# An encoder block with two attentions on one core: a hand-written VectorE order, a later meta product, another order of pair products, and keys and queries loaded a head ahead

## The chip, the cores and the metric

The kernel runs on one core of one Trainium2 chip. The metric is the device time of one execution in microseconds (us). A core has a matrix engine (PE, with its weight loads listed apart as PEld), three engines for elementwise work (DVE is VectorE, ACT is ScalarE, POOL is GpSimd) and a queue engine (SP) that issues all loads and stores here. The engines run side by side and wait for one another by semaphores; each takes its own instructions in a fixed order.

## The reference

One block of an encoder with 1024 tokens, 16 meta tokens ahead of them, and 1024 features, in fp32. Cut to its core:

```python
h = concat(meta, x)                                   # 1040 x 1024
proj = rms_norm(h, norm_mix) @ w_in                   # qa ka va | qb kb vb | ga gb
# differential attention: 4 heads, two maps each, values of 128, all 1040 keys
attn = softmax(q1 k1 + bias) - lam * softmax(q2 k2 + bias)
y_a  = rms_norm(attn @ v, subln_g) * (1 - lambda_init)
# windowed attention: 8 heads in 2 groups, a block of 128 queries sees its own block,
# one to either side, and the 16 meta keys; a sink logit joins the denominator
y_b  = softmax_with_sink(qb kb + bias) @ vb
h = h + (sigmoid(ga) * (y_a @ w_ba) + sigmoid(gb) * (y_b @ w_bb)) @ w_o
n = rms_norm(h, norm_ffn)
h = h + (silu(n @ w_g) * (n @ w_u)) @ w_d             # 2816 hidden features
out = rms_norm(h, norm_final)[meta:]
```

## The kernel before

Every fp32 operand of a product is kept as two fp32r tiles, a rounded high part and the rest (`split`, L120 to L122: ACT writes the high part, L121; POOL or DVE the low part, L122). A product is three matmuls: high by high, high by low, low by high. Matmuls have at most 512 columns.

The work around the change falls into four stages, in order of time.

**Window attention** (L320 to L390, up to about 245 us). For each group and block of 128 queries `attend_b` makes the scores (`bps`, two matmuls for each of four heads, L331), and a generator `values` makes the transposes (`bpt`, L365), their splits (`btr`: ACT L367, DVE L369), the products with the values (`bpy`, L359) and the result (ACT L380, DVE L381). The last step of `values` is the product with the 16 meta values and the result. PE's order is written out by hand here: the string `SLOTS_B` is gone through once for each block, and takes a score step ("s"), a step of `values` of the block before ("t"), the last step of `values` of the block before that ("y"), or a step of three matmuls of other projections (`more`, made by `fill_b`, "g").

**Sums for the pair products** (about 230 to 272 us). Some projections are done in pairs of 128-column blocks and two halves of the tokens and features, by a seven-product scheme in place of eight. Products 5, 6, 7 and 4 need sums of normalised inputs: `token_sums(u)` makes, for each of four groups of 128 tokens in either half, four sums of high and low part (`f`, L620), four differences (L622 to L625), and four splits into `tops` (ACT high, DVE low, L122). Meanwhile PE runs the rest of `more`. The order on DVE, ACT, POOL and SP is chosen here by the framework's scheduler.

**Pair products** (L655 to L718, about 260 to 360 us). A unit is one pair of column blocks: units 0 and 1 are the queries of the differential attention, 2 to 4 are gates. `steps_t` lists (unit, product) in PE's order, written by hand. `weights_t` makes the weight sums (`s1` and the in-place differences in `wt`, L667 to L671, DVE) and splits them into `wop_t` (ACT, POOL), up to four products ahead. `product_t` runs 12 matmuls (`pt`, L697) into a PSUM bank. Products 1, 6, 7, 4 go into one bank and 5, 3 into another, 2 into a third, each adding to what stands there. After 1, 5 and 6 ACT copies the bank (`u`, L701); after 2, 7 and 3 DVE adds the bank to a copy (L706). The results of units 0 and 1 are split once more (`qk_stage`: ACT L235, DVE L236), stored, and loaded again by the heads; those of the gates are stored.

**Heads** (L760 to L935, about 366 to 640 us). For 4 heads and 8 tiles of 128 queries: `load_a` (at a head's first tile) issues on SP the loads of the second map's queries and keys (L768, L769, L771), the first map's, and the values. `scores_a` makes scores (`aps`, L792) for the second map and then the first, with minimum, exponential and combination on DVE, ACT and POOL (L795 to L806); `turn` transposes two tiles later (`apt`, L818; split L820 to L822); `values_a` and `normed_a` make products with the values (`apy`, L831) and the norm (`apst`, `af`, `apf`, L844 to L852). The order on PE is again by hand: `SLOTS` for the first `N_MORE` tiles, `SLOTS_LAST` for the others, with "s" a score step, "t" a transpose step, "n" a step of the values or the norm, "g" a step of three matmuls of the gate projections that are left (`fill(1)`). `G_FIRST` steps run at the start, `G_HEAD` at each new head, and `HOLD` steps are kept for the end, where `while tail` runs the last values with three gate steps each.

Results of gate projections are stored by SP (L748); SP takes its instructions in order, so a store that waits holds what stands behind it.

Of the kernel before, what the change touches and what calls it, by code (L numbers as in the profile page):

```python
# [39 lines left out]
PC_BUFS = 8  # L40
PAD_T = 192
COMBINE_POOL = (0, 1, 2, 3)
SLOTS = "stgstgstgsngsnsn"
SLOTS_LAST = "stgstgstsngsnsn"
N_MORE = 13
S_BUFS = (2, 2)
AT_BUFS = 2
G_BUFS = 3
HOLD = 39
PAIRS = 3  # L50
HEADS_EARLY = 3
GT_BUFS = 4
WB_BUFS = 5
G_HEAD = 7
G_FIRST = 33

QK_BUFS = 3
W_BUFS = 2
# [2 lines left out]
V_AT = 2  # L61
S_BUFS_B = 3
B_FIRST = 6
SLOTS_B = "ysgtgsgtgtsgtgtsgtgt"
E_STEPS = 1
OP_BUFS = 8
RING_RAW = 5
# [12 lines left out]
def encoder_block(ctx: ExitStack, tc: tile.TileContext, x, meta, norm_mix, w_in, lq1, lk1, lq2, lk2,  # L80
# [7 lines left out]
    def f32(ap):  # L88
        return ap.bitcast(F32)
# [520 lines left out]
    def quad(t, kh, th, u):  # L610
        return t[:, 4 * kh:4 * kh + 4, th * 512 + u * P:th * 512 + u * P + P]

    def token_sums(u):

        cols = slice(u * P, u * P + P)
        tt = nc.vector.tensor_tensor
        f = {}
        for kh, th in ((0, 0), (0, 1), (1, 1), (1, 0)):
            f[kh, th] = pc_tile(f"f{kh}{th}_{u}").rearrange("p (c t) -> p c t", c=4)
            tt(f[kh, th], f32(quad(hT_hi, kh, th, u)), f32(quad(hT_lo, kh, th, u)), ALU.add)  # L620
        b11, b12, b21, b22 = f[0, 0], f[0, 1], f[1, 0], f[1, 1]
        tt(b12, b12, b11, ALU.subtract)  # L622
        tt(b22, b22, b12, ALU.subtract)
        tt(b11, b22, b11, ALU.subtract)
        tt(b21, b21, b22, ALU.subtract)  # L625
        for p, src in ((6, b22), (5, b12), (7, b11), (4, b21)):
            split(tops[p][:, 0, :, cols], tops[p][:, 1, :, cols], src, nc.vector)

    def moving(p, c, b):
        if p in tops:  # L630
# [2 lines left out]
        return (hT_hi, hT_lo)[b][:, 4 * kh + c, th * 512:th * 512 + 512]  # L633


    for _ in more:
        pass
    flush_v()
    for u in range(4):
        token_sums(u)  # L640
    close_psum1()
    psum_t, close_psum_t = pool("psum_t", space=PSUM)
    psum1 = psum_t
# [2 lines left out]
    units = [[C_QA + (2 * i + k) * P for k in range(2)] for i in range(2)]  # L646
    units += [gate_cols[2 * i:2 * i + 2] for i in range(PAIRS)]
    steps_t = [(u, p) for u in range(2) for p in (1, 2)]
    steps_t += [(u, p) for u in range(2) for p in (6, 5, 7, 3, 4)]
    steps_t += [(u, p) for u in range(2, len(units)) for p in (1, 2, 6, 5, 7, 3, 4)]  # L650
    raw_t, s1_t, ops_t, ps_t, u_t = {}, {}, {}, {}, {}

    def load_t(u):
# [6 lines left out]
    def weights_t(u, p):  # L660
        tt = nc.vector.tensor_tensor
        a11, a12 = (raw_t[u, kh][:, :, 0:P] for kh in range(2))
        a21, a22 = (raw_t[u, kh][:, :, P:2 * P] for kh in range(2))
        if p == 6:

            s1_t[u] = tpool.tile([P, 4, P], F32, tag="s1", name=f"s1_{u}", bufs=2)
            tt(s1_t[u], a21, a22, ALU.add)  # L667
            tt(a21, a11, a21, ALU.subtract)
            tt(a11, s1_t[u], a11, ALU.subtract)
        elif p == 3:  # L670
            tt(a12, a12, a11, ALU.subtract)  # L671
        src = s1_t.pop(u) if p == 5 else {1: a11, 2: a12, 6: a11, 7: a21, 3: a12, 4: a22}[p]
        op = wpool.tile([P, DC, P], F32R, tag=("wh", "wl")[len(ops_t) % 2], name=f"wop_t{u}_{p}", bufs=W_BUFS)
        ops_t[u, p] = op
        split(op[:, 0:4], op[:, 4:8], src, nc.gpsimd)
# [14 lines left out]
    def product_t(u, p):  # L690
        op, key = ops_t[u, p], (u, {1: 1, 6: 1, 7: 1, 4: 1, 2: 2, 5: 3, 3: 3}[p])
        if p in (1, 2, 5):
            ps_t[key] = pp_bank(f"pt_{u}_{p}")
        ps = ps_t[key]
        for c in range(4):
            for n, (a, b) in enumerate(((0, 0), (0, 1), (1, 0))):
                nc.tensor.matmul(ps, op[:, 4 * a + c], moving(p, c, b), start=(p in (1, 2, 5) and c == 0 and n == 0),  # L697
                                 stop=(p in (4, 2, 3) and c == 3 and n == 2), skip_group_check=True)
        if p in (1, 5, 6):
            u_t[u, p] = pc_tile(f"u{p}_{u}")  # L700
            nc.scalar.copy(u_t[u, p], ps)  # L701
        elif p == 4:
            result_t(u, 1, 0, ps, True)
        else:
            other = u_t.pop((u, {2: 1, 7: 5, 3: 6}[p]))
            nc.vector.tensor_tensor(other, ps, other, ALU.add)  # L706
            result_t(u, *{2: (0, 0), 7: (1, 1), 3: (0, 1)}[p], other)

    for u in range(3):
        load_t(u)  # L710
# [48 lines left out]
    for i in range(2):  # L759
        nc.gpsimd.memset(s0s[i][:, L + 2 * NM:], 0.0)  # L760

    def load_a(h):
        p = apool
        qs, ks = [None, None], [None, None]
        for m in (1, 0):
            q = qs[m] = p.tile([P, S], F32R, tag=f"q{m}", name=f"aq{h}_{m}")
            k = ks[m] = p.tile([P, 2, L], F32R, tag=f"k{m}", name=f"ak{h}_{m}")
            nc.sync.dma_start(f32(q), qa_d[h][m])  # L768
            nc.sync.dma_start(f32(k)[:, 0, :], ka_d[h][m])  # L769
            for hl in range(2):  # L770
                nc.sync.dma_start(f32(k)[64 - 64 * hl:128 - 64 * hl, 1, :], ka_d[h][m, 64 * hl:64 * hl + 64, :])  # L771
        v = p.tile([P, 2, 9, P], F32R, tag="v", name=f"av{h}")
        nc.gpsimd.memset(f32(v)[:, 0, 8, :], 0.0)
        nc.sync.dma_start(f32(v)[:, :, 0:8, :], va_d[h][:, :, 0:8, :])
        nc.sync.dma_start(f32(v)[:2 * NM, 0, 8, :], va_d[h][:2 * NM, 0, 8, :])
        nc.sync.dma_start(f32(v)[2 * NM:3 * NM, 0, 8, :], va_d[h][:NM, 1, 8, :])
        return qs, ks, v
# [102 lines left out]

    order_pe = tc.manual_schedule(engines={mybir.EngineType.PE})
    order_pe.__enter__()
    tiles, turning, tail = [], iter(()), []

    def step_tail():
        while tail and next(tail[0], True):
# [2 lines left out]
    for n in range(AH * NT + T_LAG):  # L889
        scoring, turning = iter(()), iter(())  # L890
        if n < AH * NT:
            h, t = divmod(n, NT)
            if t == 0:
                ld = load_a(h)
                if not h:
                    fill(G_FIRST)
            if t % 2 == 0:
                at_ = apool.tile([P, 9, 2, 256], F32R, tag="at", name=f"at{h}_{t}", bufs=AT_BUFS)
            s = [None, None]
            tiles.append((h, t, s, at_, ld[2]))  # L900
            scoring = scores_a(h, t, ld, s)
        if n >= T_LAG:
            turning = turn(tiles[n - T_LAG])
        if n in (NT, 2 * NT, 3 * NT):

            fill(G_HEAD - 3)
            for _ in turning:
                pass
            step_tail()
            fill(3)  # L910
        for what in SLOTS if n < N_MORE else SLOTS_LAST:
            if what == "s":
                next(scoring, None)
            elif what == "t":
                next(turning, None)
            elif what == "n":
                step_tail()
            else:
                fill(1)
        for _ in scoring:  # L920
            pass
        for _ in turning:
            pass
        if n in (1, 2):
            fill(3)
        if n >= T_LAG and tiles[n - T_LAG][1] % 2:
            tail.append(later(tiles[n - T_LAG]))
    n_gates[0] += HOLD
    while tail:
        step_tail()  # L930
        fill(3)
    order_pe.__exit__(None, None, None)
    close_apool()
    fill(1000)
# [604 lines left out]
```

## Time and profile before

| | |
|---|---|
| median of 3 runs | 1493.73 us (1493.52 to 1493.82) |
| the profiled execution | 1494.14 us, span 1492.4 us |
| PE busy | 1443.1 us, 97% of the span |
| DVE, ACT, POOL busy | 892.0, 687.9, 562.7 us |
| HBM read, written | 131.24 MB, 53.94 MB |

The span runs from the first to the last recorded instruction; the time of the execution is somewhat longer. Times in the trace are counted from the start of the span. A row of a timeline gives the start, the duration, the engine, the line of the kernel, the operation with output and inputs, and how many instructions of that kind follow each other; in brackets stands how long the engine was idle just before and what released it. A matmul's end is modelled, so that consecutive matmuls overlap in such rows. A row of waits gives the engine, what it wanted to run, whose instruction it waited for, the total, the number of times and the longest.

### The profile page before, as it was taken

The page shows a single profiled execution, that of the slowest core. Times are in us where ns is not written, and L with a number is a line of the kernel's source. Part 1 is how long each engine was busy: PE and PEld are TensorE (multiplying, and loading weights), DVE is VectorE, ACT ScalarE, POOL GpSimd, SP SyncE. Part 2 cuts the span into 40 slices and gives each one's busy share as a digit, 9 for nine tenths or more (in the row PEclk, how much of TensorE's full clock was granted, in tenths as well). Part 3 has the DMA queues.
Part 4 walks back from the last instruction along what each step waited for, and adds up shares of the span by engine and source line. Part 5 has one row for each costly group of instructions (what it writes and reads, how often), then busy time and mean ns, then how long its engine had stood idle before and what let it go on. Part 6 is the DMA issues. An engine that isn't in the chain of part 4 may idle for free.

```text
span 1492.4 us, 21014 instructions
## 1 busy us (share of the span) xinstructions
PE 1443.1 (97%) x7315; PEld 1228.8 (82%) x7315; DVE 892.0 (60%) x1635; ACT 687.9 (46%) x1296; POOL 562.7 (38%) x556
## 2 busy tenths in 40 slices
PE   8999998999999999999999999999999999999997
PEld 7988888788889898878888878888888888888886
DVE  6466668621768786813432586655555554778567
ACT  6366663432555565625533463333333333444444
POOL 4253433543332232313763325544455453000344
PEclk9999999899999999999999999999999999999999
DMA  7423324434542414147653244322333332864433
GB/s 235 90 81 105 93 79 136 134 106 126 160 130 78 122 65 144 42 146 227 206 183 113 90 126 145 124 98 98 104 106 107 106 106 106 309 224 131 134 123 139
DMA packets 154203, 193.13 MB, mean 129 GB/s; under 512 B 16288, under 2 KB 98656, under 8 KB 154096
## 3 DMA queue, kind: packets, MB, share of 16 engines
q1 hardware_dynamic: 154096, 191.78, 40.8%
q8 instruction: 58, 0.95, 0.3%
q14 instruction: 49, 0.40, 0.1%
HBM read 131.24 MB, written 53.94 MB: 124 GB/s over the span
## 4 chain that ended last, share of the span: by engine, by line
PE 77%; DMA 7%; DVE 5%; issue 4%; POOL 4%; ACT 2%; SPq 1%; POOLq 0%; ACTq 0%; DVEq 0%
PE pg L1320 28%; PE pd L1414 8%; PE pt L697 6%; PE po L1086 6%; PE pp_g L215 5%; PE aps L792 4%; PE ppa L735 4%; PE apy L831 3%; DMA ak<-ka_d 3%; POOL oa L122 3%; PE pp_qb L215 3%; PE apt L818 2%; PE bpt L365 1%; PE pp_ka L215 1%; PE pp_va L215 1%
## 5 line engine op out<-in xcount | busy, mean ns | idle before, releaser
L1320 PE MATMUL pg<-t,wop 128*128 128x512 f32 x1056 | 243.0, 389 | 1.6 <-DVE wop L122 1.6
L1320 PEld LDWEIGHTS pg<-t,wop 128*128 128x128 f32 x1056 | 198.1, 188 | 43.3 <-DVE wop L122 2.0
L122 POOL TENSOR_TENSOR wop<-wf,wop 128x512 fp32r<-128x512 f32 x118 | 158.6, 1347 | 155.3 <-ACT wop L121 141.0
L1414 PE MATMUL pd<-ob,oa 128*128 128x512 f32 x924 | 210.2, 389 | 0.9 <-DVE ob L122 0.5
L1414 PEld LDWEIGHTS pd<-ob,oa 128*128 128x128 f32 x924 | 173.3, 188 | 37.6 <-DVE ob L122 0.9
L1320 PE MATMUL pg<-b,wop 128*128 128x512 f32 x792 | 183.2, 389 | 0.0
L1320 PEld LDWEIGHTS pg<-b,wop 128*128 128x128 f32 x792 | 148.5, 188 | 30.7
L121 ACT ACTIVATE wop<-wf 128x512 fp32r<-128x512 f32 x128 | 80.3, 632 | 83.1 <-PE pg L1320 51.9
L800 ACT ACTIVATE as<-as,amn 128x1040 f32<-128x1040 f32 x64 | 74.6, 1165 | 74.8 <-DVE amn L795 65.9
L122 POOL TENSOR_TENSOR oa<-ra,oa 128x512 fp32r<-128x512 f32 x33 | 44.0, 1335 | 170.8 <-ACT oa L121 169.4
L792 PE MATMUL aps<-ak,aq 128*128 128x352 f32 (+1 forms) x384 | 91.9, 331 | 10.1 <-DMA ak<-ka_d 8.5
L121 ACT ACTIVATE oa<-ra 128x512 fp32r<-128x512 f32 x77 | 48.7, 632 | 107.7 <-PE pd L1414 51.9
L1086 PE MATMUL po<-woh,mT 128*128 128x512 f32 x384 | 88.6, 390 | 0.0
L792 PEld LDWEIGHTS aps<-ak,aq 128*128 128x128 f32 x384 | 66.9, 190 | 23.7 <-issue 6.8
L188 POOL TENSOR_TENSOR wl_c<-w_c,wh_c 128x512 fp32r<-128x512 f32 x48 | 61.1, 1295 | 61.7 <-ACT wh_c L185 61.7
L1086 PEld LDWEIGHTS po<-woh,mT 128*128 128x128 f32 x384 | 71.7, 188 | 14.7
L1144 DVE TENSOR_TENSOR s<-wf,wf 128x512 f32<-128x512 f32 x22 | 16.5, 752 | 109.0 <-DMA wf<-in_w_ff_up_dram 54.5
L122 POOL TENSOR_TENSOR wop_t<-wt,wop_t 128x512 fp32r<-128x512 f32 x30 | 46.6, 1557 | 63.7 <-ACT wop_t L121 62.2
L345 POOL TENSOR_SCALAR bs<-bs,bdn 128x432 f32<-128x432 f32 (+1 forms) x64 | 36.9, 596 | 89.0 <-DVE bdn L343 57.8
L215 PE MATMUL pp_g<-hT_hi,wh_c 128*128 128x512 f32 x160 | 68.7, 430 | 0.0
L803 POOL TENSOR_SCALAR as<-as,adn,neglam 128x1040 f32<-128x1040 f32 x32 | 38.9, 1215 | 73.2 <-DVE adn L801 68.8
L215 PE MATMUL pp_g<-hT_hi,wl_c 128*128 128x512 f32 x160 | 63.3, 395 | 0.0
(279 smaller groups left out, 3173.5 us busy)
## 6 DMA issues: line engine op xcount, KB each, us to landing
ra<-aop SPq DMA_DIRECT2D x77, 256.0 KB, 2.6
w_c<-in_w_in_dram SPq DMA_DIRECT2D x25, 512.0 KB, 4.3
wf<-in_w_ff_gate_dram SPq DMA_DIRECT2D x24, 512.0 KB, 3.6
wf<-in_w_ff_up_dram SPq DMA_DIRECT2D x24, 512.0 KB, 3.5
aop<-as SPq DMA_DIRECT2D x44, 256.0 KB, 2.1
aop<-c SPq DMA_DIRECT2D x33, 256.0 KB, 2.0
gt<-g_d SPq DMA_DIRECT2D x32, 256.0 KB, 3.2
wt<-in_w_in_dram SPq DMA_DIRECT2D x10, 512.0 KB, 4.6
```

What stands on the lines that cost most here:

```text
L121: nc.scalar.activation(hi, src, AF.Copy)
L122: lo_eng.tensor_tensor(lo, src, f32(hi), ALU.subtract)
L188: (lo_eng or nc.gpsimd).tensor_tensor(wl[:, c], w[:, c], f32(wh[:, c]), ALU.subtract)
L215: nc.tensor.matmul(ps[:, :n], a[:, c, :], b[:, c, at:at + n], start=(c == 0 and i == 0), stop=(c == DC - 1 and i == 2))
L697: nc.tensor.matmul(ps, op[:, 4 * a + c], moving(p, c, b), start=(p in (1, 2, 5) and c == 0 and n == 0), stop=(p in (4, 2, 3) and c == 3 an ...
L735: nc.tensor.matmul(ps, w[:, a, j, :], src(j, b, tk), start=(j == 0 and n == 0), stop=(j == 3 and n == 2))
L792: nc.tensor.matmul(ps[:, :n], qs[m][:, t * P:(t + 1) * P], ks[m][:, vv, k0:k0 + n], start=(vv == 0), stop=(vv == 1))
L800: nc.scalar.activation(s[m][:, 0:L], s[m][:, 0:L], AF.Exp, bias=low, scale=-1.0, accum_out=dn[:, m:m + 1])
L831: nc.tensor.matmul(py[:, cols], v[:kp, a, k, :], at_[:kp, k, b, :], start=(k == 0 and j == 0), stop=(k == 8))
L1086: nc.tensor.matmul(ps, mT[:, c, a, t * P:(t + 1) * P], wos[q, c][:, b], start=(c == 0 and n == 0), stop=(c == DC - 1 and n == 2))
L1320: nc.tensor.matmul(ps, op[:, x, c, :], b[:, y, c, :], start=(p in (1, 2, 5) and c == 0 and n == 0), stop=(p in (4, 2, 3) and c == 3 and n ...
L1414: nc.tensor.matmul(ps[u], oa[:, a, u * P:(u + 1) * P], ob[:, b, :], start=(p in (1, 2, 5) and j == 0 and k == 0), stop=(p in (2, 3, 4) and ...
```

## The change

- In the window stage the string of slots has the last values step ("y") behind the first score step and the first projection step, no longer ahead of them.
- `token_sums` becomes a generator of single DVE operations. DVE's order is written out by hand for this stretch: one operation of the sums after each of three in four steps of `more`, and the rest behind. The splits run in the order 5, 6, 7, 4.
- The pair products run 5, 3 and then 6, 7, 4. For units 0 and 1 the two 5, 3 pairs come first. The sums and differences of weights that were made at product 6 are made at product 5. The result that was formed after product 3 is formed after product 6, from the bank of 5 and 3 and the copy of 6.
- `load_qk` loads one map's queries and keys. The second map's tiles have two buffers, and those of the next head are loaded at a head's fifth tile; the first map's and the values are loaded at the head's first tile as before.
- The slot strings of the heads have their values steps at the end; `SLOTS` holds for 4 tiles and no longer for 13; three more gate steps run at the start, seven more are kept for the end. The kept steps are released at the last tile of queries, three run beside each of the two last transposes, and two instead of three beside each last values step.

```diff
--- before.py
+++ after.py
@@ -40,19 +40,19 @@
 PC_BUFS = 8
 PAD_T = 192
 COMBINE_POOL = (0, 1, 2, 3)
-SLOTS = "stgstgstgsngsnsn"
-SLOTS_LAST = "stgstgstsngsnsn"
-N_MORE = 13
+SLOTS = "stgstgstsgsgsnnn"
+SLOTS_LAST = "stgstgstsgssnnn"
+N_MORE = 4
 S_BUFS = (2, 2)
 AT_BUFS = 2
 G_BUFS = 3
-HOLD = 39
+HOLD = 46
 PAIRS = 3
 HEADS_EARLY = 3
 GT_BUFS = 4
 WB_BUFS = 5
 G_HEAD = 7
-G_FIRST = 33
+G_FIRST = 36
 
 QK_BUFS = 3
 W_BUFS = 2
@@ -61,7 +61,7 @@
 V_AT = 2
 S_BUFS_B = 3
 B_FIRST = 6
-SLOTS_B = "ysgtgsgtgtsgtgtsgtgt"
+SLOTS_B = "sgytgsgtgtsgtgtsgtgt"
 E_STEPS = 1
 OP_BUFS = 8
 RING_RAW = 5
@@ -613,18 +613,22 @@
     def token_sums(u):
 
         cols = slice(u * P, u * P + P)
-        tt = nc.vector.tensor_tensor
+
+        def tt(*args):
+            nc.vector.tensor_tensor(*args)
+
         f = {}
         for kh, th in ((0, 0), (0, 1), (1, 1), (1, 0)):
             f[kh, th] = pc_tile(f"f{kh}{th}_{u}").rearrange("p (c t) -> p c t", c=4)
             tt(f[kh, th], f32(quad(hT_hi, kh, th, u)), f32(quad(hT_lo, kh, th, u)), ALU.add)
+            yield
         b11, b12, b21, b22 = f[0, 0], f[0, 1], f[1, 0], f[1, 1]
-        tt(b12, b12, b11, ALU.subtract)
-        tt(b22, b22, b12, ALU.subtract)
-        tt(b11, b22, b11, ALU.subtract)
-        tt(b21, b21, b22, ALU.subtract)
-        for p, src in ((6, b22), (5, b12), (7, b11), (4, b21)):
+        for out, x, y in ((b12, b12, b11), (b22, b22, b12), (b11, b22, b11), (b21, b21, b22)):
+            tt(out, x, y, ALU.subtract)
+            yield
+        for p, src in ((5, b12), (6, b22), (7, b11), (4, b21)):
             split(tops[p][:, 0, :, cols], tops[p][:, 1, :, cols], src, nc.vector)
+            yield
 
     def moving(p, c, b):
         if p in tops:
@@ -633,11 +637,16 @@
         return (hT_hi, hT_lo)[b][:, 4 * kh + c, th * 512:th * 512 + 512]
 
 
-    for _ in more:
+    order_dve = tc.manual_schedule(engines={mybir.EngineType.DVE})
+    order_dve.__enter__()
+    sums = chain.from_iterable(token_sums(u) for u in range(4))
+    for i, _ in enumerate(more):
+        if i % 4 < 3:
+            next(sums)
+    flush_v()
+    for _ in sums:
         pass
-    flush_v()
-    for u in range(4):
-        token_sums(u)
+    order_dve.__exit__(None, None, None)
     close_psum1()
     psum_t, close_psum_t = pool("psum_t", space=PSUM)
     psum1 = psum_t
@@ -646,8 +655,9 @@
     units = [[C_QA + (2 * i + k) * P for k in range(2)] for i in range(2)]
     units += [gate_cols[2 * i:2 * i + 2] for i in range(PAIRS)]
     steps_t = [(u, p) for u in range(2) for p in (1, 2)]
-    steps_t += [(u, p) for u in range(2) for p in (6, 5, 7, 3, 4)]
-    steps_t += [(u, p) for u in range(2, len(units)) for p in (1, 2, 6, 5, 7, 3, 4)]
+    steps_t += [(u, p) for u in range(2) for p in (5, 3)]
+    steps_t += [(u, p) for u in range(2) for p in (6, 7, 4)]
+    steps_t += [(u, p) for u in range(2, len(units)) for p in (1, 2, 5, 3, 6, 7, 4)]
     raw_t, s1_t, ops_t, ps_t, u_t = {}, {}, {}, {}, {}
 
     def load_t(u):
@@ -661,7 +671,7 @@
         tt = nc.vector.tensor_tensor
         a11, a12 = (raw_t[u, kh][:, :, 0:P] for kh in range(2))
         a21, a22 = (raw_t[u, kh][:, :, P:2 * P] for kh in range(2))
-        if p == 6:
+        if p == 5:
 
             s1_t[u] = tpool.tile([P, 4, P], F32, tag="s1", name=f"s1_{u}", bufs=2)
             tt(s1_t[u], a21, a22, ALU.add)
@@ -699,12 +709,12 @@
         if p in (1, 5, 6):
             u_t[u, p] = pc_tile(f"u{p}_{u}")
             nc.scalar.copy(u_t[u, p], ps)
-        elif p == 4:
+        if p == 4:
             result_t(u, 1, 0, ps, True)
-        else:
-            other = u_t.pop((u, {2: 1, 7: 5, 3: 6}[p]))
-            nc.vector.tensor_tensor(other, ps, other, ALU.add)
-            result_t(u, *{2: (0, 0), 7: (1, 1), 3: (0, 1)}[p], other)
+        elif p in (2, 6, 7):
+            other = u_t.pop((u, {2: 1, 6: 6, 7: 5}[p]))
+            nc.vector.tensor_tensor(other, ps_t[u, 3] if p == 6 else ps, other, ALU.add)
+            result_t(u, *{2: (0, 0), 7: (1, 1), 6: (0, 1)}[p], other)
 
     for u in range(3):
         load_t(u)
@@ -759,16 +769,18 @@
     for i in range(2):
         nc.gpsimd.memset(s0s[i][:, L + 2 * NM:], 0.0)
 
-    def load_a(h):
+    def load_qk(h, m):
+        q = apool.tile([P, S], F32R, tag=f"q{m}", name=f"aq{h}_{m}", bufs=1 + m)
+        k = apool.tile([P, 2, L], F32R, tag=f"k{m}", name=f"ak{h}_{m}", bufs=1 + m)
+        nc.sync.dma_start(f32(q), qa_d[h][m])
+        nc.sync.dma_start(f32(k)[:, 0, :], ka_d[h][m])
+        for hl in range(2):
+            nc.sync.dma_start(f32(k)[64 - 64 * hl:128 - 64 * hl, 1, :], ka_d[h][m, 64 * hl:64 * hl + 64, :])
+        return q, k
+
+    def load_a(h, first):
         p = apool
-        qs, ks = [None, None], [None, None]
-        for m in (1, 0):
-            q = qs[m] = p.tile([P, S], F32R, tag=f"q{m}", name=f"aq{h}_{m}")
-            k = ks[m] = p.tile([P, 2, L], F32R, tag=f"k{m}", name=f"ak{h}_{m}")
-            nc.sync.dma_start(f32(q), qa_d[h][m])
-            nc.sync.dma_start(f32(k)[:, 0, :], ka_d[h][m])
-            for hl in range(2):
-                nc.sync.dma_start(f32(k)[64 - 64 * hl:128 - 64 * hl, 1, :], ka_d[h][m, 64 * hl:64 * hl + 64, :])
+        qs, ks = zip(load_qk(h, 0), first)
         v = p.tile([P, 2, 9, P], F32R, tag="v", name=f"av{h}")
         nc.gpsimd.memset(f32(v)[:, 0, 8, :], 0.0)
         nc.sync.dma_start(f32(v)[:, :, 0:8, :], va_d[h][:, :, 0:8, :])
@@ -880,7 +892,7 @@
 
     order_pe = tc.manual_schedule(engines={mybir.EngineType.PE})
     order_pe.__enter__()
-    tiles, turning, tail = [], iter(()), []
+    tiles, turning, tail, ahead = [], iter(()), [], None
 
     def step_tail():
         while tail and next(tail[0], True):
@@ -891,14 +903,18 @@
         if n < AH * NT:
             h, t = divmod(n, NT)
             if t == 0:
-                ld = load_a(h)
+                ld = load_a(h, ahead or load_qk(h, 1))
                 if not h:
                     fill(G_FIRST)
+            if t == 4 and h < AH - 1:
+                ahead = load_qk(h + 1, 1)
             if t % 2 == 0:
                 at_ = apool.tile([P, 9, 2, 256], F32R, tag="at", name=f"at{h}_{t}", bufs=AT_BUFS)
             s = [None, None]
             tiles.append((h, t, s, at_, ld[2]))
             scoring = scores_a(h, t, ld, s)
+        if n >= AH * NT:
+            fill(3)
         if n >= T_LAG:
             turning = turn(tiles[n - T_LAG])
         if n in (NT, 2 * NT, 3 * NT):
@@ -923,12 +939,13 @@
             pass
         if n in (1, 2):
             fill(3)
+        if n == AH * NT - 1:
+            n_gates[0] += HOLD
         if n >= T_LAG and tiles[n - T_LAG][1] % 2:
             tail.append(later(tiles[n - T_LAG]))
-    n_gates[0] += HOLD
     while tail:
         step_tail()
-        fill(3)
+        fill(2)
     order_pe.__exit__(None, None, None)
     close_apool()
     fill(1000)
```

## What is predicted

> **What bounds the kernel now.** I read the page's head and busy times first, then the waits of TensorE (PE), then the windows of the three stages that the change touches, then the timeline at the longest waits. The page, its span and its first busy line:
>
> ```profile
> span 1492.4 us, 21014 instructions
> PE 1443.1 (97%) x7315; PEld 1228.8 (82%) x7315; DVE 892.0 (60%) x1635; ACT 687.9 (46%) x1296; POOL 562.7 (38%) x556
> ```
>
> PE sets the time: 1492.4 − 1443.1 = 49.3 us of idle is all that reordering can win, except for what the clock gives. The change alters no matmul count, so I count only idle time removed and added, and half-clock time. The waits of PE over the whole run (us in total, times, longest):
>
> ```profile
> PE aps L792 <- DMA ak<-ka_d: 8.5, 8, 1.7
> PE bpy L359 <- DVE btr L369: 7.1, 13, 0.8
> PE pt L697 <- DVE tops L122: 3.3, 1, 3.3
> PE apt L818 <- DVE as L806: 2.5, 2, 1.7
> PE bpy L359 <- ACT btr L367: 0.7, 1, 0.7
> PE aps L792 <- DVE amn L795: 0.7, 1, 0.7
> PE apf L852 <- POOL af L847: 0.3, 1, 0.3
> ```
>
> The first, second and fifth rows are targets of the change: head loads and the meta product. The windows: window attention, the sums before the pair products, the pair products, and two clock windows at the start of head 1 (columns after the busy times: granted PE clock, DMA share, GB/s):
>
> ```profile
> 125.00:245.00 120.00, 114.69 (x697) 103.98 (x696) 81.87 (x192) 72.36 (x170) 41.95 (x63) 1.00 0.36 102
> 245.00:272.40 27.40, 19.31 (x90) 15.58 (x88) 27.40 (x44) 13.54 (x26) 10.64 (x4) 0.91 0.21 59
> 272.40:365.00 92.60, 92.60 (x398) 76.25 (x399) 28.57 (x36) 31.48 (x54) 44.55 (x37) 0.97 0.42 126
> 441.70:445.10 3.40, 1.40 (x8) 1.18 (x9) 0.57 (x3) 1.08 (x2) 2.03 (x2) 1.00 0.35 128
> 445.10:448.50 3.40, 3.40 (x15) 3.20 (x14) 1.28 (x6) 0.00 (x0) 1.21 (x1) 0.50 0.55 160
> ```
>
> VectorE (DVE) is busy for all 27.40 us of the second stage, which sets its end; in the third PE is busy throughout, with nothing to win and everything to lose.
>
> **Meta product behind scores.** Timeline of PE in one block, and the pieces of the chain just before its wait:
>
> ```profile
> 184.65 0.63 PE L359 MATMUL bpy<-btr,vb 128*128 128x512 f32 x2
> 186.08 0.50 PE L359 MATMUL bpy<-btr,vb 128*128 128x512 f32 x1 [0.80 <-DVE btr L369]
> 186.42 0.55 PE L331 MATMUL bps<-kb,qb 128*128 128x432 f32 x2
> 186.81 0.34 PE L215 MATMUL pp_va<-hT_hi,wh_c 128*128 128x384 f32 x1
> 186.99 0.34 PE L215 MATMUL pp_va<-hT_lo,wh_c 128*128 128x384 f32 x1
> ...
> 185.35 0.69 DVE btr L369
> 186.04 0.04 issue
> ```
>
> A modelled matmul overlaps its follower: the pace is a start each 0.23 us (48 matmuls in 11.06 us, row further down). After 184.65 the third start would be 185.11 and is 186.08, so this stall cost 0.97 for 0.80 of listed idle, 0.17 more; and the next start is 0.34 later, not 0.23, 0.11 more. So each stall of PE costs its idle and about 0.27.
>
> The change puts one score step (two matmuls, 186.42 to 186.81: 0.39) and one projection step (three at 0.18: 0.54) ahead of the meta product. 0.93 us covers the longest such wait, 0.80. The 13 + 1 waits sum to 7.8, with 14 × 0.27 = 3.8: 11.6 at most. The evacuation of the block's result, behind the meta product, becomes 0.93 later, and the next score's DVE operation now stands between; I keep 9 (7 to 11.6).
>
> **Pair products.** Before, a unit's products run 6, 5, 7, 3, 4, alternating between two PSUM banks, so each copy or sum of a bank has another product's matmuls (12 × 0.23 = 2.8 us) as cover. Now they run 5, 3 in one bank and 6, 7, 4 in the other: 3 must wait for the copy of 5, 7 for the copy of 6, 4 for the sum of 7. The cover is gone at three places in each of five units, 15 new stalls. Rows: groups of the stage, the pace, and one copy whose product's matmuls were the first 24 of the 48:
>
> ```profile
> L706 DVE TENSOR_TENSOR u<-pt,u 128x512 f32<-128x512 f32 x14 | 9.6, 688 | 29.6 <-PE pt L697 29.5
> L701 ACT COPY u<-pt 128x512 f32<-128x512 f32 x13 | 7.6, 586 | 18.3 <-PE pt L697 18.3
> ...
> 286.01 11.06 PE L697 MATMUL pt<-tops,wop_t 128*128 128x512 f32 x48
> ...
> 291.67 0.59 ACT L701 COPY u<-pt 128x512 f32<-128x512 f32 x1 [0.58 <-PE pt L697]
> ```
>
> The 24th matmul starts at 286.01 + 23 × 0.227 = 291.23; the copy starts 0.44 later and takes 0.59; PE restarts 0.04 after a release (the issue row above). Start to start that is 1.07 where 0.23 was: 0.84, and 0.11 for the next matmul, 0.95. A sum instead of a copy (0.69): 1.05. One of the 15 stands apart below; the others: 9 × 0.95 + 5 × 1.05 = 13.8. The lower bound leaves out the 0.11: 12.3. The upper has ACT or DVE occupied by another operation when the product ends (first rival).
>
> The Trainium skill (Perfetto Trace Analysis, Optimizing Tensor Performance: Matmuls) says that matmul groups should rotate through different PSUM banks, so that one's evacuation overlaps the next one's matmuls. It speaks against this order, and the 92.60 busy of 92.60 in the stage's window agrees with it; it gives no price.
>
> **Start of the pair products.** Timelines of PE, POOL, DVE and ACT, in this order:
>
> ```profile
> 272.36 11.02 PE L697 MATMUL pt<-tops,wop_t 128*128 128x512 f32 x35 [3.29 <-DVE tops L122]
> ...
> 267.56 4.20 POOL L122 TENSOR_TENSOR wop_t<-wt,wop_t 128x512 fp32r<-128x512 f32 x1 [8.67 <-ACT wop_t L121]
> ...
> 230.72 4.89 DVE L620 TENSOR_TENSOR f<-hT_hi,hT_lo 128x512 f32<-128x512 f32 x8
> 238.93 0.69 DVE L667 TENSOR_TENSOR s<-wt,wt 128x512 f32<-128x512 f32 x1 [1.52 <-DMA wt<-in_w_in_dram]
> 275.60 1.76 DVE L122 TENSOR_TENSOR tops<-f,tops 128x512 fp32r<-128x512 f32 x1
> 278.49 0.68 DVE L706 TENSOR_TENSOR u<-pt,u 128x512 f32<-128x512 f32 x1
> ...
> 279.20 0.64 ACT L235 ACTIVATE qk_stage<-u 128x512 fp32r<-128x512 f32 x1 [6.48 <-DVE u L706]
> 279.74 0.57 ACT L701 COPY u<-pt 128x512 f32<-128x512 f32 x1
> ```
>
> The first product with token sums starts when the last part of its operand is split. From the first sum to that split DVE has 62 operations in the old order (operand 6), 60 in the new (operand 5): 2 × 0.61 = 1.2 us earlier. Against that, the weight sum that waited 1.52 for its load stands three places earlier, so waits 3 × 0.61 = 1.8 more, and two weight sums that wait on POOL's splits stand earlier in an order that can no longer be changed around them: 0 to 2. So 0.6 to 2.6 us later; I take 0.6.
>
> The first copy of product 5 is worse. On ACT it stands behind the splits of two earlier results, which wait for DVE. Before, the second result's sum ended at 278.49 + 0.68 = 279.17, 6.8 us after 272.36, with six operations since; ACT's split followed at 279.20 and the copy ended at 280.31. It cost nothing, as the next product used the other bank. In the new order eight operations stand between: 6.8 + 2 × 0.61 = 8.0 after the first matmul, the copy ends 0.04 + 0.54 + 0.57 later, at 9.2. The product's twelve matmuls (35 in 11.02 us: 0.31 each) are over at 3.8, so PE waits 5.4. The slow matmuls that follow 272.36 in the old run are partly replaced by this wait, at 0.31 − 0.23 = 0.08 each for some 15: −1.2. Together 0.6 + 5.4 − 1.2 ≈ 5 (2.7 if the DVE operations all take 0.61 as at 230.72; 8 with the late weight sums).
>
> DVE's 1.76 where 0.69 is usual falls beside POOL's splits. The Trainium skill (SBUF — State Buffer, "There are two physically separate sides", on the shared port pair) has such pairs lock each other out for a whole instruction; the 4.20 beside 1.72 on POOL agrees.
>
> **Heads.** PE and SP (the queue that issues loads):
>
> ```profile
> 381.61 0.40 PE L792 MATMUL aps<-ak,aq 128*128 128x352 f32 x1 [1.27 <-DMA ak<-ka_d]
> 442.98 0.39 PE L792 MATMUL aps<-ak,aq 128*128 128x352 f32 x1 [1.69 <-DMA ak<-ka_d]
> 575.33 0.40 PE L792 MATMUL aps<-ak,aq 128*128 128x352 f32 x1 [1.46 <-DMA ak<-ka_d]
> ...
> 429.09 0.32 SPq L768 DMA_DIRECT2D aq<-qa_d  x1
> 432.43 0.33 SPq L768 DMA_DIRECT2D aq<-qa_d  x1
> 434.46 7.53 SPq L748 DMA_DIRECT2D g_d<-gate_stage  x2
> ...
> 633.01 1.20 PE L818 MATMUL apt<-ident,as 128*128 128x128 f32 x9 [1.73 <-DVE as L806]
> ```
>
> Loading the second map four tiles ahead takes its DMAs off the head's start, and the first map's are issued 432.43 − 429.09 = 3.3 us earlier, more than the 1.46 of 575.33. Head 0 has nothing to load ahead; three more gate steps (9 × 0.23 = 2.1) cover its 1.27. All eight waits go: 8.5 + 8 × 0.27 = 10.7. The window 441.7 to 445.1, in which PE was busy for 1.40 of 3.40, is followed by one at clock 0.50, half of 3.40 lost: 1.7. Sum 12.4. The new order of a tile's slots packs the values steps at its end: between −0.7 (the wait on amn goes) and +5 (seven more of its size); I take +2, since these waits are rare now. The three fills beside the last transposes cover 1.73 and 0.3: −2 (0 to −2.6). Moved gate steps keep their work. Heads: −12.4.
>
> **Sum.** −9 + 13.8 + 5 − 12.4 = −2.6 against the profiled run's 1494.14; the median of the runs shown is 1493.73, 0.4 lower. 1493.73 − 2.6 = 1491.1; I say 1491.0. A difference under 0.2% (3.0 us) is about what a measurement of this kernel can't tell from none.
>
> **Rivals.**
> The forecast's own range: the terms' spreads (2, 2, 3 and 3 us) together about 4.5, so 1486.5 to 1495.5. Chance 0.55, of which 0.27 is past −3.0 and 0.28 inside.
>
> Slower, by queues behind the copies: the copies and sums that PE now waits for stand in ACT's and DVE's fixed orders beside weight splits (0.63) and other sums (0.69). With one ahead at each of the 14 places: 9 × 0.63 + 5 × 0.69 = 9.1, net +6.5, 1500.2. It turns slower than the bound from nine places on. For it: ACT's copy at 279.74 stood behind a split; against: ACT is busy 31.48 of 92.60. Chance 0.16.
>
> Faster: the first copy finds DVE ahead, since the sums begin earlier and run without gaps, and the start costs nothing: −2.6 − 5 = −7.6, 1486.1. Against it stands DVE's 27.40 of 27.40. Chance 0.13.
>
> Slower, by the queue of SP: in order of issue, a gate's store holds it for 7.53 us (434.46). If stores hold the early loads or the first map's, two thirds of 12.4 are lost: +5.7, 1499.4. Chance 0.06; four tiles of lead speak against.
>
> The change doesn't do what it says at the meta product: the wait moves with it, since the transposes of one block end later than the cover: +9, net +6.4, 1500.1. Chance 0.05.
>
> A clock that dips again: 15 stalls close together might bring 15 windows of 3.40 at 0.50, 1.7 each: +25, 1516. Against it: in 125 to 245 with its 14 stalls the granted clock was 1.00. Chance 0.05. The Trainium skill (TensorE: Matmul & The Clock Gate, A second HAM failure mode: psum-queue depth-cycling) tells of micro-idles between matmul groups that make the gate swing; by that rule the pair products would lose those 25 us.
>
> **Chances.** Faster 0.27 + 0.13 = 0.40; same 0.28; slower 0.16 + 0.06 + 0.05 + 0.05 = 0.32. The range takes the forecast's own and the rivals from 1486.1 to 1500.2, and leaves out the clock's case and the tails: 1485.5 to 1500.5.
>
> **What would show it.** After: no row of aps waiting on ak; the bpy waits gone, or a few tenths; some 15 new rows of pt waiting on ACT's u or DVE's u, each near 0.8 of idle; a first wait of 4 to 6 us on ACT's u soon after the first product; the span of the pair products longer by about 14. I am wrong if the pt waits are under 5 or over 20 us together without the first, if load waits of over 3 us stay, or if new rows at the clock of 0.5 stand in the pair products.

## The result, and the profile after

The changed kernel takes 1511.32 us (median of 4 runs, 1510.74 to 1515.94) against 1493.78 for the kernel before beside it (1493.52 to 1496.09): a ratio of 1.0121, 95% interval 1.0098 to 1.0143. It is 17.5 us slower, outside the predicted range of 1485.5 to 1500.5. Its profiled execution, head and busy times:

```profile
span 1509.0 us, 21023 instructions
PE 1450.9 (96%) x7315; PEld 1229.7 (81%) x7315; DVE 890.0 (59%) x1635; ACT 689.7 (46%) x1296; POOL 560.2 (37%) x556
```

The same matmuls, 7.8 us more of PE busy and 8.8 more of idle. Of the busy time, 3.3 more lie in the pair products, at the same granted clock as before (windows below), and 3.5 in the heads, where two windows at half clock (402.90 to 409.70, further down) stand in place of one. The longest waits of PE in the stages of the change:

```profile
PE pt L707 <- ACT u L711: 11.9, 10, 5.8
PE pv_va L253 <- DVE qk_stage L233: 4.9, 1, 4.9
PE pv_va L253 <- DVE va_stage L557: 4.7, 1, 4.7
PE pt L707 <- DVE u L716: 3.9, 5, 0.8
PE aps L804 <- DMA ak<-ka_d: 2.8, 3, 1.2
PE aps L804 <- DVE at L834: 2.6, 9, 0.3
...
PE aps L804 <- DVE amn L807: 1.5, 2, 1.3
...
PE bpy L359 <- DVE btr L369: 0.7, 3, 0.3
```

The meta product's wait has shrunk from 7.1 to 0.7 and the load waits from 8.5 to 2.8, as meant. In return stand 15 waits of the pair products on copies and sums, one wait of 4.9 of a value transpose (`pv_va`), and nine waits on `at`. The 4.7 on `va_stage` was 1.5 before; it falls at 242.72, in the stretch of the sums, whose end DVE sets (busy for 40.99 of 45.64 us).

Windows cut at the same events in both traces, before first: from the last meta product to the first full product of a token sum, the pair products, and from there to the branch products (span, PE busy, PEld, DVE, ACT, POOL, clock, DMA share, GB/s):

```profile
229.00:272.36 43.36, 35.27 (x190) 31.42 (x189) 40.73 (x64) 19.13 (x37) 14.20 (x6) 0.95 0.40 120
272.36:360.46 88.10, 88.10 (x372) 71.75 (x373) 28.61 (x36) 29.70 (x51) 41.71 (x32) 0.97 0.39 117
360.46:668.81 308.35, 293.06 (x1803) 263.50 (x1801) 207.16 (x600) 155.91 (x285) 84.82 (x102) 0.99 0.38 114
```

```profile
222.50:268.14 45.64, 36.65 (x189) 32.97 (x188) 40.99 (x62) 17.71 (x33) 11.42 (x5) 0.93 0.39 115
268.14:375.32 107.18, 91.38 (x372) 69.95 (x373) 29.23 (x38) 32.10 (x56) 42.30 (x32) 0.97 0.32 98
375.32:685.53 310.21, 296.58 (x1803) 263.32 (x1801) 205.24 (x600) 157.88 (x285) 85.39 (x102) 0.99 0.37 114
```

Up to the last meta product the changed kernel is 6.5 us ahead (222.5 against 229.0). Then it loses 2.3, 19.1 and 1.9: together 16.8, for 16.6 of span. The last number is the surprise; 12.4 were to be won there.

The long wait, timelines of PE and ACT and two pieces of the chain after it:

```profile
268.14 2.79 PE L707 MATMUL pt<-tops,wop_t 128*128 128x512 f32 x11 [1.96 <-DVE tops L122]
276.74 0.80 PE L707 MATMUL pt<-hT_hi,wop_t 128*128 128x512 f32 x1 [5.80 <-ACT u L711]
...
275.58 0.63 ACT L235 ACTIVATE qk_stage<-u 128x512 fp32r<-128x512 f32 x1 [2.80 <-DVE u L716]
276.12 0.57 ACT L711 COPY u<-pt 128x512 f32<-128x512 f32 x1
...
276.74 7.45 PE pt L707 x24
284.21 0.59 ACT u L711
```

The copy that product 3 needs stands behind a split, which waits for DVE: PE idles 5.80 us. From then on the chain alternates between 12, 24 or 48 matmuls and one copy or sum, where before it was one piece of PE.

At the heads, SP's queue, two waits of PE, the piece of the chain ahead of the first, and the two windows around it:

```profile
386.65 0.34 SPq L775 DMA_DIRECT2D aq<-qa_d  x1
...
395.17 0.82 SPq L558 DMA_DIRECT2D va_d<-va_stage  x1
...
397.02 5.18 SPq L548 DMA_DIRECT2D ka_d<-qk_stage  x2
...
395.17 8.97 DMA va_d<-va_stage
...
405.38 0.40 PE L253 MATMUL pv_va<-ident,vt_va 128*32 128x128 f32 x1 [4.87 <-DVE qk_stage L233]
...
402.90:406.30 3.40, 0.92 (x4) 0.93 (x5) 1.54 (x6) 1.63 (x3) 0.00 (x0) 0.54 0.86 298
406.30:409.70 3.40, 3.40 (x16) 3.40 (x15) 3.04 (x12) 1.41 (x3) 0.46 (x2) 0.50 0.47 130
...
447.56 0.32 SPq L775 DMA_DIRECT2D aq<-qa_d  x1
...
449.94 0.33 SPq L775 DMA_DIRECT2D aq<-qa_d  x1
...
460.59 0.40 PE L804 MATMUL aps<-ak,aq 128*128 128x352 f32 x1 [1.20 <-DMA ak<-ka_d]
```

The early load for head 1 is not issued at tile 4 of head 0 but at 386.65, before the first score of head 0: its second buffer is free from the start, and the scheduler that orders SP puts it right behind head 0's own loads. The stores of head 3's projections, which are made at the start of head 0, come behind it: the one issued at 395.17 takes 8.97 us, its staging buffer comes free late, ACT and DVE fill it only then, and PE waits 4.87 us. The later early loads have to wait for a buffer; that is released at the end of a head, and so the load for head 2 (447.56) goes out ahead of the first map's load of head 1 (449.94), which is late as before.

### The profile page after: what moved, and what is told of

The parts are those of the page before. It is cut to its first block, busy times and chain, and to the rows that moved or that the text cites. A ratio compares the mean times of both kernels' runs of the same rounds, so it can differ in the third digit from the quotient of the medians.

```text
span 1509.0 us, 21023 instructions
## 1 busy us (share of the span) xinstructions
PE 1450.9 (96%) x7315; PEld 1229.7 (81%) x7315; DVE 890.0 (59%) x1635; ACT 689.7 (46%) x1296; POOL 560.2 (37%) x556
## 4 chain that ended last, share of the span: by engine, by line
PE 76%; DVE 7%; DMA 5%; issue 5%; POOL 4%; ACT 2%; SPq 1%; POOLq 0%; DVEq 0%; ACTq 0%
PE pg L1337 27%; PE pd L1431 8%; PE pt L707 6%; PE po L1103 6%; PE pp_g L215 5%; PE ppa L745 4%; PE aps L804 3%; PE apy L843 3%; POOL oa L122 3%; PE pp_qb L215 2%; PE pp_va L215 2%; PE pp_ka L215 1%; PE bpy L359 1%; PE bpt L365 1%; DMA ak<-ka_d 1%
## 5 line engine op out<-in xcount | busy, mean ns | idle before, releaser
L122 POOL TENSOR_TENSOR wop_t<-wt,wop_t 128x512 fp32r<-128x512 f32 x30 | 41.0, 1368 | 78.8 <-ACT wop_t L121 78.8
L707 PE MATMUL pt<-tops,wop_t 128*128 128x512 f32 x240 | 59.5, 396 | 9.3 <-DVE u L716 3.9
```

The source lines that it names most:

```text
L122: lo_eng.tensor_tensor(lo, src, f32(hi), ALU.subtract)
```

## Experiments

Each time is compared with that of the kernel before, run beside it: 1493.8 us for the first four experiments, 1493.7 for the next four, 1495.2 for the last three. "Heads" is the stretch from the last pair product to the branch products: 308.35 us before, 310.21 after.

**The pair products back in the old order, the rest of the change kept.** In the list of steps (weight sums and results go with it):

```diff
-    steps_t += [(u, p) for u in range(2) for p in (5, 3)]
-    steps_t += [(u, p) for u in range(2) for p in (6, 7, 4)]
-    steps_t += [(u, p) for u in range(2, len(units)) for p in (1, 2, 5, 3, 6, 7, 4)]
+    steps_t += [(u, p) for u in range(2) for p in (6, 5, 7, 3, 4)]
+    steps_t += [(u, p) for u in range(2, len(units)) for p in (1, 2, 6, 5, 7, 3, 4)]
```

> The changed kernel with the pair products back in the order 6, 5, 7, 3, 4 (the code of the kernel before for the list of steps, the weight sums and the results; the order of the splits of the token sums stays 5, 6, 7, 4). Theory: the 14 short waits on copies and sums (10.0 us of idle in the changed kernel's trace, 13.8 with 0.27 each) and the long one (5.8) go, and nothing else changes: 1511.3 - 19 = 1492 us, and no rows of pt waiting on ACT's or DVE's u. Rival: the time comes back as waits at the start of head 0, whose loads then start earlier against stores that are still running: 1498 to 1505 us.

Measured: 1495.74 us, ratio 1.0004 (0.9989 to 1.0019). The last matmul of the pair products starts at 354.4 instead of 374.9 us, 20.5 earlier (19 expected, and the start of this run was 1.0 faster); no row of pt waiting on u is left. But 5 of it came back at head 0, as the rival said; the time lies between the two forecasts. The wait there, and the piece of the chain ahead of it:

```profile
PE pv_va L253 <- DVE qk_stage L233: 9.7, 1, 9.7
...
377.85 10.63 DMA va_d<-va_stage
```

**The first early load held back.** Before the load of head 1's second map, its buffers take a value that depends on a score of tile 3:

```diff
+    held = [apool.tile([P, S], F32R, tag="q1", name="held_q", bufs=2),
+            apool.tile([P, 2, L], F32R, tag="k1", name="held_k", bufs=2)]
...
+            if t == 4 and not h:
+                late = tiles[-1][2][1][:, 0:1]
+                nc.gpsimd.tensor_copy(held[0][:, 0:1], late)
+                nc.gpsimd.tensor_copy(held[1][:, 0, 0:1], late)
```

> The changed kernel with the early load of head 1's second map held back to tile 4 of head 0 (its buffers take a value of a score of tile 3 first, on GpSimd). Theory of the collision: in the changed kernel the four transfers were issued at 386.65 us, right behind head 0's own, and kept the stores and the weight loads back; without them the wait of 4.9 us of pv_va and the two half-clock windows after it (1.7 each) go: -8.5, 1502.8 us. Rival theory (the three more gate steps at head 0's start fill the staging buffers too early): the wait stays within 1 us, 1511 us.

Measured: 1509.65 us, ratio 1.0103 (1.0082 to 1.0123). The wait of pv_va on `qk_stage` is gone, so the early load is its cause. The time gained 1.7 only. The heads took 307.01, 3.2 less:

```profile
377.62:684.63 307.01, 296.46 (x1803) 262.79 (x1801) 205.25 (x600) 158.10 (x285) 85.35 (x104) 0.99 0.37 116
```

My 8.5 was too high: of the two half-clock windows PE was idle for most of the first, a new one followed at head 1's load wait, and a wait of 1.1 of apt came up. Of the 3.2, 2.4 were lost again in the profiled run's pair products (109.58 against 107.18 us), although every engine has the same order up to there: so much varies from run to run.

**G_FIRST back at 33.** 

> The changed kernel with G_FIRST back at 33, the early load where it is. Theory of the collision: the wait of pv_va on DVE's qk_stage stays near 4.9 us (at most 1 us less, moved by the 2 us that three steps take), and the scores of head 0 wait for their load as before (1.3 us): 1511 to 1513 us. Rival theory (the gate steps are the cause): the wait falls below 1 us and the time to 1503 to 1506 us.

Measured: 1520.05 us, ratio 1.0164 (1.0142 to 1.0186). The wait stayed and grew, and the load waits with it, more than I expected:

```profile
PE aps L804 <- DMA ak<-ka_d: 9.1, 5, 3.0
PE pv_va L253 <- DVE qk_stage L233: 6.0, 1, 6.0
```

The three steps are not its cause. Why their loss costs 9 us, with load waits at all later heads too, is not explained. One difference is on record and was not tested: at heads 1 and 2 a weight load of the gates (L181) now goes out at 445.74 and 521.38, next to the heads' own loads; in the changed kernel these went at 439.18 and 507.04, over 6 us ahead of them.

**All early loads held back.** As above, with `h < AH - 1` for `not h`; at later heads the tiles that take the value are those of the head's own second map of the head before (`held = [ld[0][1], ld[1][1]]` before each early load).

> The changed kernel with every early load held back to tile 4 of the head ahead, so that the first map's load at a head's start has no other load ahead of it on SP. Theory: in the changed kernel the early load for the head after next is issued at the change of heads (447.56 us), ahead of the first map's own (449.94), and so the first map's landed as late as before (460.46); with this the waits of 1.2, 0.8 and 0.8 us go as well, each with 0.27: against the run with only the first load held, -3.6 us, about 1499 us. Rival: the first map's tile has one buffer and its load is late by that alone: the waits stay, the time is that of the run with only the first load held.

Measured: 1502.08 us, ratio 1.0050 (1.0034 to 1.0067): 9.2 less than the changed kernel, and 7.6 less than the run with the first load held, where 3.6 were expected. SP's queue, PE's waits and the heads:

```profile
421.85 0.34 SPq L775 DMA_DIRECT2D aq<-qa_d  x1
...
446.01 0.32 SPq L775 DMA_DIRECT2D aq<-qa_d  x1
...
PE aps L804 <- DVE at L834: 3.1, 11, 0.3
...
PE pv_va L253 <- DVE qk_stage L233: 1.6, 1, 1.6
...
PE aps L804 <- DMA ak<-ka_d: 0.2, 1, 0.2
...
374.50:677.07 302.57, 294.36 (x1803) 261.19 (x1801) 205.57 (x600) 157.95 (x285) 86.04 (x108) 1.00 0.38 118
```

Now the early load goes out at 421.85, in the midst of head 0, and the first map's at 446.01 with nothing ahead of it: 0.2 of the load waits is left. The rival, that one buffer makes the first map late anyhow, falls. Head 0 waits 1.6 for pv_va although no early load is out by then; in the run with the first load held it did not. So that much of this wait comes and goes without the early load.

**Both faults undone** (old order of products and all early loads held). 

> The changed kernel with both faults undone: pair products in the old order 6, 5, 7, 3, 4, and every early load held back to tile 4 of the head ahead. If the two causes add up: against the run with the old order alone (1495.7), the wait of pv_va of 9.7 with 0.3 and its two half-clock windows (3) go, and the load waits of 1.2, 0.8 and 0.9 with 0.27 each: about -16, some -2 back from waits that come up in their place (1.6 and 1.1 in the run with all loads held): 1482 us, range 1479 to 1486. Rival: with the shorter pair products head 0's own loads start earlier and collide with the last stores, and a wait of several us stays there: 1488 to 1494.

Measured: 1483.17 us, ratio 0.9931 (0.9913 to 0.9949), as the sum of the causes said. No wait of over 0.4 us is left in the heads' trace; they took 299.65 us, with these left:

```profile
PE aps L803 <- DVE at L833: 3.1, 11, 0.4
...
355.40:655.05 299.65, 293.91 (x1801) 261.26 (x1800) 205.28 (x600) 158.20 (x285) 86.20 (x108) 1.00 0.38 119
```

**The same with the sums left to the scheduler.** `token_sums` and the loop over `more` are again those of the kernel before.

> The same, with DVE's order for the token sums no longer by hand: the sums as a plain function after the projections, and the order left to the scheduler as in the kernel before (splits 6, 5, 7, 4). Theory: the order by hand cost the 2.3 us that lie between the last meta product and the first product of a token sum (45.7 against 43.4): this is 2 to 3 us faster than with the order by hand. Rival: the order by hand gained, and that stretch was longer for the shift of the window stage alone (loads of weights at a fixed time): this is 1 to 3 us slower. Within 1 us: it does not matter.

Measured: 1483.19 us, ratio 0.9934 (0.9917 to 0.9950): no difference. From the last meta product to the first full product of a sum, first in this run, then in the one ahead:

```profile
221.80:265.88 44.08, 35.40 (x189) 31.45 (x188) 41.17 (x64) 19.24 (x37) 13.60 (x6) 0.96 0.40 119
222.10:268.36 46.26, 36.76 (x189) 32.85 (x188) 41.46 (x63) 18.11 (x33) 11.61 (x5) 0.93 0.38 113
```

So the order by hand does cost 2.2 us there, but in the run without it head 0 waits for pv_va (1.9, with a half-clock window behind it), and nothing is left of the gain. That this wait comes of the order is not shown: the next run has the order by hand and the same wait.

**The same as "both faults undone", with the old slots** (`SLOTS`, `SLOTS_LAST`, `N_MORE` 13, `HOLD` 39). 

> The same as the kernel with both faults undone, with the slot strings, N_MORE and HOLD of the kernel before. Theory: the new strings cost the short waits of aps on at (11 times 0.28, 3.1 us in the run with all loads held, 0.27 more each: 6 us), of which the old strings bring back 1 to 2 in other waits: 4 us faster. Rival: the new strings keep the loads' cover and the old ones bring back waits on amn and on loads: 2 to 5 us slower.

Measured: 1477.20 us, ratio 0.9896 (0.9881 to 0.9911), 6.0 less. All 11 waits of aps on at are gone. The two traces' heads differ by 2.3 only; the run with the old slots has a wait of 1.2 with two half-clock windows behind it:

```profile
PE apst L855 <- DVE amn L806: 1.2, 1, 1.2
...
353.98:651.34 297.36, 291.51 (x1801) 264.49 (x1800) 206.67 (x600) 156.59 (x285) 86.72 (x108) 0.99 0.37 116
608.40:615.20 6.80, 6.65 (x24) 5.70 (x24) 4.06 (x12) 1.57 (x4) 2.41 (x3) 0.54 0.00 0
```

**The new window slots alone,** in the kernel before (`SLOTS_B`). 

> The kernel before with the new string of slots in the window stage alone. Theory: 14 waits go, the last meta product comes 7.5 us earlier as in the changed kernel, and DVE starts its token sums as much earlier, so all of it arrives at the first product of a token sum: 1493.8 - 7.5 = 1486.3 us. Rival: the sums wait for the weight loads and POOL's splits, which do not move, and 2 to 5 us of it are lost there: 1488 to 1492 us.

Measured: 1487.79 us, ratio 0.9953 (0.9933 to 0.9972): −5.9 us: 1.5 slower than the forecast and just under the rival's range. Of the meta product's waits 0.7 is left, the last product comes at 222.2; 0.8 is lost up to the sums' product (44.11 us against 43.36), and the heads then took 309.2, 0.9 more.

**Two units in turn.** All early loads held; units 0 and 1 keep the change's order, but product by product in turn, and units 2 to 4 have the old one:

```diff
-    steps_t += [(u, p) for u in range(2) for p in (5, 3)]
-    steps_t += [(u, p) for u in range(2) for p in (6, 7, 4)]
-    steps_t += [(u, p) for u in range(2, len(units)) for p in (1, 2, 5, 3, 6, 7, 4)]
+    steps_t += [(u, p) for p in (5, 3, 6, 7, 4) for u in range(2)]
+    steps_t += [(u, p) for u in range(2, len(units)) for p in (1, 2, 6, 5, 7, 3, 4)]
```

> The changed kernel with all early loads held back, and the pair products in a third order: units 0 and 1 run the order of the change (5, 3, 6, 7, 4), but product by product in turn, so that another unit's product lies between two that share a bank; units 2 to 4 run 6, 5, 7, 3, 4 as before. Theory (what costs is the missing cover, not the order of the products in a bank): all 14 short waits go, as in the run with the old order (1483.2 us); of the long wait on the first copy, 5.8, one more product of 2.8 to 3.7 is cover, 2 to 3 stay: 1484 to 1487 us. Rival (an accumulation that follows a read of its bank costs by itself): waits on u of some 0.7 stay in units 0 and 1, six of them, 1488 us and more.

Measured: 1485.52 us, ratio 0.9939 (0.9918 to 0.9961). The waits on copies and sums:

```profile
PE pt L706 <- DVE u L715: 0.6, 1, 0.6
PE pt L706 <- ACT u L710: 0.4, 1, 0.4
```

Within a bank the products follow each other as in the change, and two small waits are left instead of five and the long one. The run is 2.3 us slower than the one with the old order, within what the runs vary. For units 0 and 1, the only ones that ran so, it is the missing cover that costs, not the order within a bank. This is the rule of the Trainium skill that the prediction cited (Perfetto Trace Analysis, Matmuls: rotate through different banks), here with a price.

**The new order of the products alone,** in the kernel before. 

> The kernel before with the new order of the pair products alone (list of steps, weight sums, results); DVE's order left to the scheduler, token sums split 6, 5, 7, 4. Theory: 14 short waits, 13.8 with 0.27 each, and the long wait on the first copy, 5 to 6: 1493.8 + 19 = 1513 us (1510 to 1515). Rival (the long wait came of the sums by hand, which put the first units' sums behind all splits): the long wait is below 3 us and the time 1508 to 1510.

Measured: 1513.83 us, ratio 1.0129 (1.0102 to 1.0156):

```profile
PE pt L698 <- ACT u L702: 10.0, 10, 3.9
...
PE pt L698 <- DVE u L707: 3.9, 5, 0.8
```

One part alone costs 18.7 us. The long wait is 3.9 here, between theory and rival; another wait, of 3.0 for POOL's weight split, has moved ahead of it. So the order of the sums by hand is not what makes it.

**What is left as a gain.** The kernel before with the new window slots, early loads held to tile 4, G_FIRST 36, and the fills beside the last transposes (three) and values steps (two); everything else as before. 

> What the runs so far leave of the change as a gain: the kernel before with the new slots of the window stage, early loads of the second map held to tile 4 with two buffers, 36 first gate steps, three gate steps beside the last transposes and two beside each last values step; sums, pair products, slot strings, N_MORE and HOLD as before. If the parts add up: the run with old slots (1477.2) with the sums planned by the scheduler, which made no difference elsewhere: 1477 us, 1475 to 1479. Rival: the order by hand starts head 0 better (its first stage was 1.4 us later and the heads 3.4 shorter), 1479 to 1481.

Measured: 1476.64 us (5 runs), ratio 0.9874 (0.9853 to 0.9895): 18.5 us faster than the kernel before, as the sum of the parts said.

## Why the prediction was wrong, step by step

**Meta product: right.** Predicted −9 (7 to 11.6), measured −7.5 up to the last meta product: 6.5 ahead, after a start that was 1.0 slower, as the last projection of window keys (`pp_kb`) shows. The granted clock from 17.0 to 20.4 us was 0.50 there and 0.79 before; where the first half-clock windows fall varies between runs.

**Short waits: right.** 13.8 predicted. The trace has 6.1 + 3.9 of idle in these 14; with 0.27 each, an estimate of the prediction, 13.8. The chain shows it without that estimate:

```profile
305.35 11.36 PE pt L707 x48
...
327.64 11.38 PE pt L707 x48
```

A unit of 84 matmuls now takes 22.3 us from start to start. At the pace of before, 0.23 each, it takes 19.3, so its three stalls cost 3.0.

**Start of the pair products: right in mechanism, 2.6 too low.** About 5 were predicted and 7.6 measured: 2.3 up to the sums' product, and 19.1 − 13.8 = 5.3 behind it. The wait on the first copy was 5.80 where 5.4 was predicted, by the chain that was named (a split on ACT that waits for DVE). The sums' own end was to come 0.6 later and came 2.3 later, within the 0.6 to 2.6 given; the order by hand costs most of that (44.08 against 46.26). In this stretch DVE's waits for weight loads rose from the 1.52 of before to 3.4 in two waits, by as much as the prediction had counted.

**Heads: the step that failed,** −12.4 predicted and +1.9 measured: 14.3 of the miss of about 20 (the start is 2.6 and the meta product 2.5 of the rest). Three parts of it were wrong.

- "Loading the second map four tiles ahead takes its DMAs off the head's start": I took the place in the program for the place in the queue. PE's order is by hand in this stage; SP's is not, and a load whose buffer is free goes as soon as the scheduler finds room. It fell on head 0's start. There the DMA engines had no idle time for four more transfers; they were busy throughout already before (first row; the second is after):

```profile
360.40:390.00 29.60, 27.18 (x169) 26.19 (x168) 11.08 (x32) 9.94 (x17) 6.70 (x9) 1.00 1.00 258
...
375.30:407.00 31.70, 26.83 (x165) 26.39 (x164) 9.17 (x28) 8.47 (x15) 6.62 (x8) 0.94 0.99 283
```

  "Head 0 has nothing to load ahead" left these transfers out of the sum. Holding the first load back removed the new wait of 4.9. The rival on SP's queue had the right engine and the wrong culprit: not a gate's store held the loads back, the early loads held the others.
- "The first map's are issued 3.3 us earlier": that interval was the wait for the first map's only buffer (in the trace of before a score of PE, its last reader, releases the load), and in the changed kernel an early load took the place ahead of it. Holding all early loads removed these waits and took 9.2 us off; the heads then took 302.57, 5.8 less than before.
- Slots: +2 taken, −0.7 to +5 given. With the old ones the time falls by 6.0 between the medians, and the heads of the two traces differ by 2.3, with two half-clock windows (some 3 us) against the old ones. The 11 waits of 0.28 with 0.27 each would be 6.0; how much of the 6.0 is theirs alone stays open.

With loads held and the old slots the heads are 11.0 shorter than before, and by estimate some 3 more without the half-clock windows at 608 (6.80 us at 0.54): together 14, where the terms for waits removed (12.4 and 2) make 14.4. They were sized right, but they were claims on a kernel in which the loads go where the text puts them.

None of the three signs that the prediction named for being wrong came clearly: the pt waits are 10.0 without the first one, the load waits 2.8, and the half-clock stretch in the pair products lies at their start, as before. A new wait for a store was not on its list. The rivals on queues behind copies and on a dipping clock did not come either: no wait of the 14 is over 0.8, and the granted clock of the pair products was 0.97 before and after. There the rule of the Trainium skill on micro-idles (TensorE: Matmul & The Clock Gate, psum-queue depth-cycling) did not show: from 280.40 to 375.30, with all 14 short stalls, the granted clock was 1.00.

## What to carry to other kernels

A load that is written earlier goes as early as its buffer and its queue allow, not where the line stands: before pricing it, look up its place in the compiled order of its queue, and what it then stands in front of. Where it must come later than its buffer, give it something to wait for, a value from the work beside which it should run. Products that share an accumulator bank and need a copy in between cost about 1 us each here (128x512, a copy of 0.59 or a sum of 0.69) without another product between them; for two units, running them in turn gave nearly all of that cover (1485.5 us against 1483.2).

## What the runs showed that was not expected

A buffer more made a load harmful: with the shorter pair products the same early load cost a wait of 9.7 us in place of 4.9. And a wait of PE is followed by a stretch at half clock often, but not always: 1.9 us at pv_va had one window behind it in the run with the sums left to the scheduler and none in the run with the old slots, the 14 stalls of 0.7 to 0.8 had none, and the wait of 1.2 at 608 had two.
